# Global attention scores: three products of 64 rows, two key tiles at a time, in place of two products of 128 rows

## The chip, the cores and the metric

The kernel runs on one core of one Trainium2 chip. The metric is the device time of one execution in microseconds (us), and the time before is the median of three runs. PE is TensorE (PEld its weight loads), DVE is VectorE, ACT is ScalarE, POOL is GpSimd, SP is SyncE.

## The reference

One layer of a diffusion backbone over 1024 latent tokens and 256 context tokens, with 1024 channels. After a modulated projection there are two attention branches of 8 query heads and 2 key heads each (64 channels per head): branch A sees a window of 128 tokens to either side, branch B sees all 1024 latent keys, and both see the 256 context keys. A gated merge, a LayerNorm, a convolutional feed-forward block and a second LayerNorm follow. The part that the change touches is branch B:

```python
def _gqa_scores(q, k):
    return jnp.einsum("bqhgd,bkhd->bhgqk", q, k).astype(jnp.float32) * (HEAD_DIM ** -0.5)

def _global_attention(q, k_all, v_all):
    def one_block(i):
        q_blk = lax.dynamic_slice_in_dim(q, i * BLOCK, BLOCK, axis=1)
        p = jax.nn.softmax(_gqa_scores(q_blk, k_all), axis=-1)
        return _gqa_values(p, v_all)
```

Everything is float32.

## The kernel before

**Numbers in two parts.** Matrix products run on the type fp32r (`R32`), a float32 with a shortened mantissa. A float32 number is therefore split into a high part and a low part (`split`, L80): the high part is the rounded copy, and the low part is what is left. A product of two numbers then is high by high, high by low and low by high (`mm3`, L89: three matmuls), with low by low left out.

**Scores of the global branch.** A head has only 64 channels, so the high and the low part of a query fit one above the other on 128 rows. `qprep` (L479) makes two such tiles per unit: `q1` with the high part on rows 0 to 63 and the low part on rows 64 to 127, and `q2` with the two halves swapped. The keys lie the same way in `KL[h]` (128 rows, 1024 key columns; `KL[0]`, `KL[1]` for the windowed branch, `KL[2]`, `KL[3]` for the global one). `qk` (L494) then takes two matmuls of 128 rows, `q1` (L496) and `q2` (L497), and their sum holds all four products, low by low among them. One score tile `s` of a head has 1024 columns in two PSUM banks, so a head takes four matmuls of 512 columns (L520 and L521 call `qk` for each half).

**Units.** Attention is done in 32 units (`Unit`, L466): branch, block of 128 queries, group of four heads. Units 0 to 15 are windowed, 16 to 31 global. A global unit has `context` and `cxp` (scores against the context keys `KC`, tile `sx`, still with `qk`), four times `lat` (scores against the latent keys; then DVE scales them and takes the minimum, L545, and ACT takes the exponential, L547), and `value_steps`: transposes of the probabilities (L604, tile `ptr`), their split on ACT and DVE or POOL (L622, L623, L84, L87), and the products with the values (L634, L635, tile `av`). `self.kt` lists the key tiles in the order of the score columns, and `av_step` picks the value tile by it. Beside units 18 to 30 stand the matmuls of the first branch's output projection (tile `b`, L90 to L92). `s` has two buffers of two banks, `pt` (for `ptr`, `sx`, `b`) has three banks, `av` one.

**Keys.** `kv_post` (L423) prepares one tile of 128 tokens at a time: rotary embedding and norm, a split of all four key heads into `ks` on DVE (L450), four transposes on PE into `ktr` (L456), four copies into `KL` (L459, on ACT, for the last tile on DVE).

**A check inside the kernel.** In unit 3 of the windowed branch the kernel transposes one block of probabilities a second time as float32 (tile `both`, L609), copies it (L612), subtracts it from the first transpose (L613, tile `differ`) and adds the difference, times 1e30, to the unit's output (L655).

**What sets the order.** The projections up to the gates and the start of the merge are written in the order in which they run. From `loads.close()` (L832) on, keys and attention included, a scheduler decides the order of each engine's instructions from dependencies, priorities and its own costs; every engine then works through its list in that order. The stages behind attention come out in the same order before and after the change.

Of the kernel before, what the change touches and what calls it, by code (L numbers as in the profile page):

```python
# [7 lines left out]
F32 = mybir.dt.float32  # L8
R32 = mybir.dt.float32r
# [4 lines left out]
P = 128  # L14
# [55 lines left out]
def layer_kernel(  # L70
# [343 lines left out]
        q_evac(1, t, acc[t], bias_qb)  # L414

    KL, KC, VT = [], [], []

    def kv_alloc():
        KL.extend(ht(f"KL{h}", dt=R32) for h in range(4))
# [3 lines left out]
    def kv_post(t, kv):  # L423
        st = {}
        kb = kv[:, 128:256].rearrange("p (h d) -> p h d", d=HD)

        def s1():
            vt = VT[t // 2][:, t % 2]
            v3 = kv[:, 256:512].rearrange("p (h d) -> p h d", d=HD)
            nc.scalar.copy(vt[:, :, 0:HD], v3)  # L430
            tp = pw(f"ktp{t}")
            st["tp"] = tp = [tp[:, n * P:(n + 1) * P] for n in range(4)]
            st["ss"] = rms_scale(kb, 2, f"k{t}", tp[3])
            if t < NT:
                st["tb"] = ph1.tile([P, 2, HD], F32, tag="tb", name=f"tbk{t}", bufs=4)
                gfold(st["tb"], 1, t, nc.vector)
                rope(nc.vector, kv[:, 0:128], kv[:, 0:128], 2, ropec[:, t], ropes[:, t], f"ka{t}", tp[0], tp[1])
            nc.gpsimd.tensor_tensor(out=vt[:, :, HD:P], in0=v3, in1=vt[:, :, 0:HD].bitcast(F32), op=ALU.subtract)

        def s2():  # L440
            rms_apply(kb, 2, st["ss"])
            tp = st["tp"]
            if t < NT:
                tb = st["tb"]
                rope(nc.vector, kv[:, 128:256], kv[:, 128:256], 2, tb[:, 0], tb[:, 1], f"kb{t}", tp[2], tp[3])
            else:
                nc.gpsimd.tensor_tensor(out=kb, in0=kb, in1=bc(gcol[:, 1], 2), op=ALU.mult)
            st["ks"] = ks = pw(f"ks{t}", (P, 4, P), R32)
            k3 = kv[:, 0:256].rearrange("p (h d) -> p h d", d=HD)
            split(k3, ks[:, :, 0:HD], ks[:, :, HD:P], nc.vector, nc.vector)  # L450

        def s3():
            ks = st["ks"]
            tr = acc_tile(f"ktr{t}", R32).rearrange("p (h q) -> p h q", h=4)
            for h in range(4):
                nc.tensor.transpose(tr[:, h], ks[:, h], identr)  # L456
            if t < NT:
                for h in range(4):
                    (nc.vector.tensor_copy if t == NT - 1 else nc.scalar.copy)(KL[h][:, t * P:(t + 1) * P], tr[:, h])  # L459
            else:  # L460
                nc.scalar.copy(KC[0][:, :, (t - NT) * P:(t - NT + 1) * P], tr)
        return [s1] + [lambda: None] * GAP + [s2, s3]
# [3 lines left out]
    class Unit:  # L466
        def __init__(self, br, i, g):
            self.br, self.i, self.g = br, i, g
            self.id = f"{br}_{i}_{g}"
            if br == 1:  # L470
                self.k0, self.w, self.nc_ = 0, T, 2
                self.kt = list(range(10))
            else:
                w = [j for j in (i - 1, i, i + 1) if 0 <= j < NT]
                self.k0, self.w, self.nc_ = w[0] * P, len(w) * P, 1
                self.kt = w + [8, 9]
            self.n = br * 2 * NT + i * 2 + g
# [16 lines left out]
        def qk(self, o, h, ks, stop=True):  # L494
            hs = slice(h * P, (h + 1) * P)
            nc.tensor.matmul(o, self.q[0][:, hs], ks, start=True, stop=False)  # L496
            nc.tensor.matmul(o, self.q[1][:, hs], ks, start=False, stop=stop)  # L497

        def begin(self):
            self.nm = small(f"nm_{self.id}", (P, 4))  # L500
            self.sm = small(f"sm_{self.id}", (P, 4))
            self.other = negsink[:, self.g * 4:self.g * 4 + 4]
# [4 lines left out]
        def lat(self, h):  # L507
# [9 lines left out]
                self.qk(s[:, 256:512], h, KC[0][:, kh])  # L517
                o = s
            elif self.br == 1:
                for c in (0, 512):  # L520
                    self.qk(s[:, c:c + 512], h, KL[kh][:, c:c + 512])  # L521
                o = s
            else:
                w = self.w
# [70 lines left out]
        def value_steps(self):  # L595
# [5 lines left out]
            def tr_step(n):  # L601
# [2 lines left out]
                    i = nc.tensor.transpose(tr[:, h * P:(h + 1) * P], self.bits[:, h, n * P:(n + 1) * P], identr)  # L604
                    tc.add_manual_dep(i.ins, self.owner, data, reason="the row's words are read under another type")
                tr = tr.bitcast(F32)
                if nm == "0_3_0" and n == 0:
                    both = pt_tile("both")
                    i = nc.tensor.transpose(both[:, 0:P], self.bits[:, 0, 0:P].bitcast(F32), ident)  # L609
                    tc.add_manual_dep(i.ins, self.owner, data, reason="the row's words are read under another type")  # L610
                    self.differ = att.tile([P, P], F32, tag="rb", name="differ", bufs=2)
                    nc.vector.tensor_copy(self.differ, both[:, 0:P])  # L612
                    nc.vector.tensor_tensor(out=self.differ, in0=tr[:, 0:P], in1=self.differ, op=ALU.subtract)  # L613
                hi = att.tile([P, 512], R32, tag="pth", name=f"pth{nm}_{n}", bufs=4)
                lo = att.tile([P, 512], R32, tag="ptl", name=f"ptl{nm}_{n}", bufs=4)
                pooled = n in POOL_LO[self.br] and not last and (self.br or 2 <= 2 * self.i + self.g < 2 * NT - 3)
# [20 lines left out]
            def out_step():  # L637
# [13 lines left out]
                                     in0=low[0:HD].rearrange("p (a b q) -> p a b q", b=2, q=P)[:, :, h],  # L651
                                     in1=up.rearrange("p (a b q) -> p a b q", b=2, q=P)[:, :, h], op=ALU.add)
                (nc.vector if last else nc.gpsimd).tensor_tensor(out=ot, in0=ot, in1=self.rb, op=ALU.mult)
                if self.id == "0_3_0":
                    nc.vector.scalar_tensor_tensor(out=ot[:, 0], in0=self.differ, scalar=1e30, in1=ot[:, 0],  # L655
                                                   op0=ALU.mult, op1=ALU.add)
                hf = self.i // 4
                qs = slice((self.i % 4) * P, (self.i % 4 + 1) * P)
                split(ot, otile(self.br, hf, 0, self.g)[:, :, qs], otile(self.br, hf, 1, self.g)[:, :, qs],
# [1295 lines left out]
```

## Time and profile before

| | before |
|---|---|
| median of 3 runs (lowest to highest) | 1539.59 us (1539.46 to 1540.71) |
| profiled execution | 1539.04 us, of which the span of the trace is 1537.3 us |
| PE busy | 1510.2 us, 98% of the span |
| DVE, ACT, POOL busy | 77%, 51%, 49% of the span |
| global attention, units 16 to 31 | from 465 to 728 us of the span |

The profile is of one execution. Its page gives the busy time of each engine, the span in 40 slices, the chain of work that ended last, and the costliest groups of instructions; the trace behind it can be asked for single instructions, waits and windows of time. A matmul's duration in it includes its way through the array, so that neighbours overlap in time: what one matmul costs in a full stream is the distance from its start to the next one's start.

### The profile page before, as it was taken

To read this page: it belongs to the slowest core of one execution; us is meant where nothing else is said; L and a number is where in the kernel's file an instruction comes from. 1 tells how busy PE (TensorE), PEld (TensorE's weight loads), DVE (VectorE), ACT (ScalarE), POOL (GpSimd) and SP (SyncE) were. 2 spreads that over 40 slices of the span, in tenths; PEclk is the share of its full clock that TensorE was granted. 3 is DMA by queue.
4 is the path that set the end of the run, shared out by engine and by line. 5 is a ranking of instruction groups with operands and counts; after the bars stand their busy time and mean duration, and the time that the engine had idled before them with its cause. 6 is when DMAs were issued, how large, how long until landed. Compare 5 with 4: busy or idle time off the path is not lost.

```text
span 1537.3 us, 22216 instructions
## 1 busy us (share of the span) xinstructions
PE 1510.2 (98%) x7805; PEld 1265.8 (82%) x7805; DVE 1177.7 (77%) x1764; ACT 789.1 (51%) x1303; POOL 749.7 (49%) x727
## 2 busy tenths in 40 slices
PE   9999999999999999999999999999999999999997
PEld 7888888887787888887888998888888888888887
DVE  6677986538788788778865888888888888657884
ACT  5322222448888777677333554444444444435552
POOL 0356522415666777776223446666677774121121
PEclk9999999999999999999999999999999999999999
DMA  9777672322223677563550322333344447996721
GB/s 370 265 243 246 206 253 89 105 75 68 57 80 87 150 177 156 137 158 89 209 165 21 114 86 96 110 110 110 110 110 110 110 110 224 343 272 210 254 101 55
DMA packets 114399, 232.09 MB, mean 151 GB/s; under 512 B 13200, under 2 KB 28048, under 8 KB 114192
## 3 DMA queue, kind: packets, MB, share of 16 engines
q1 hardware_dynamic: 99056, 201.82, 39.3%
q0 software_dynamic: 10400, 20.19, 8.7%
q10 hardware_dynamic: 4832, 8.68, 1.5%
q8 instruction: 61, 1.00, 0.3%
q14 instruction: 50, 0.41, 0.1%
HBM read 179.45 MB, written 65.86 MB: 160 GB/s over the span
## 4 chain that ended last, share of the span: by engine, by line
PE 90%; POOL 3%; DVE 3%; ACT 2%; issue 2%; DMA 0%; SPq 0%; DVEq 0%; POOLq 0%; ACTq 0%
PE ptr L604 4%; PE p L90 4%; PE p L92 4%; PE p L91 4%; PE g L90 4%; PE g L92 4%; PE g L91 4%; PE av L634 3%; PE av L635 3%; PE b L90 3%; PE b L91 3%; PE b L92 3%; PE s L496 2%; PE s L497 2%; PE c L90 2%; PE c L91 2%
## 5 line engine op out<-in xcount | busy, mean ns | idle before, releaser
L623 DVE TENSOR_TENSOR ptl<-ptr,pth 128x512 fp32r<-128x512 f32 x195 | 128.8, 686 | 25.8 <-ACT pth L622 24.2
L547 ACT ACTIVATE p<-p,nm 128x1280 f32<-128x1280 f32 (+2 forms) x128 | 139.5, 1091 | 15.7 <-DVE p L545 14.6
L87 DVE TENSOR_TENSOR ld<-rd,hd 128x1024 fp32r<-128x1024 f32 x77 | 95.6, 1260 | 49.8 <-ACT hd L82 47.7
L622 ACT CAST pth<-ptr 128x512 fp32r<-128x512 f32 x195 | 110.9, 588 | 42.6 <-PE ptr L604 36.6
L82 ACT CAST hd<-rd 128x1024 fp32r<-128x1024 f32 x77 | 79.5, 1049 | 82.9 <-PE p L92 55.5
L604 PEld LDWEIGHTS ptr<-identr,pb 128*128 128x128 f32 x944 | 97.8, 141 | 22.6 <-ACT pb L550 3.1
L604 PE MATMUL ptr<-identr,pb 128*128 128x128 f32 x944 | 105.8, 243 | 2.3 <-ACT pb L550 1.3
L87 POOL TENSOR_TENSOR wlg<-wg,whg 128x512 fp32r<-128x512 f32 x32 | 46.8, 1471 | 123.6 <-ACT whg L82 84.8
L635 PE MATMUL av<-ptl,VT 128*128 128x512 f32 x236 | 98.3, 417 | 7.3 <-POOL ptl L87 7.1
L634 PE MATMUL av<-pth,VT 128*128 128x512 f32 x236 | 102.5, 434 | 2.7 <-ACT side L646 1.3
L90 PE MATMUL p<-hd 128*128 128x512 f32 x264 | 103.5, 392 | 0.0
L92 PE MATMUL p<-hd,ld 128*128 128x512 f32 x264 | 102.8, 389 | 0.0
L91 PE MATMUL p<-ld,hd 128*128 128x512 f32 x264 | 102.7, 389 | 0.0
L90 PE MATMUL g<-hh,whg 128*128 128x512 f32 x256 | 99.9, 390 | 0.0
L92 PE MATMUL g<-hh,wlg 128*128 128x512 f32 x256 | 99.6, 389 | 0.0
L91 PE MATMUL g<-hl,whg 128*128 128x512 f32 x256 | 99.6, 389 | 0.0
L545 DVE TENSOR_SCALAR_CACHE_REDUCE p<-s,cvt,nmc 128x1024 f32<-128x1024 f32 x64 | 84.1, 1317 | 8.2 <-PE s L497 8.1
L496 PE MATMUL s<-KL,q 128*128 128x512 f32 (+2 forms) x192 | 74.8, 389 | 1.2 <-DVE p L545 1.2
L497 PE MATMUL s<-KL,q 128*128 128x512 f32 (+2 forms) x192 | 72.5, 377 | 0.0
L793 ACT ACTIVATE sg<-g,bgc 128x512 f32<-128x512 f32 x32 | 22.0, 687 | 96.2 <-PE g L92 91.5
L82 ACT CAST wS<-s 128x512 fp32r<-128x512 f32 x76 | 45.3, 620 | 46.9 <-POOL s L1254 46.2
L82 ACT CAST wA<-ru 128x512 fp32r<-128x512 f32 x57 | 35.5, 623 | 63.6 <-PE d L92 34.8
(443 smaller groups left out, 4884.7 us busy)
## 6 DMA issues: line engine op xcount, KB each, us to landing
wml<-in_wmodT_dram SPq DMA_DIRECT2D x48, 512.0 KB
ru<-in_w_up_dram SPq DMA_DIRECT2D x38, 512.0 KB
rd<-td SPq DMA_DIRECT2D x55, 256.0 KB
rd<-sd SPq DMA_DIRECT2D x44, 256.0 KB
rd<-in_w_dn_dram SPq DMA_DIRECT2D x33, 256.0 KB
wm<-in_wmodT_dram SPq DMA_DIRECT2D x16, 512.0 KB
wg<-in_w_g_dram SPq DMA_DIRECT2D x32, 256.0 KB
sgd<-sg ACTq DMA_DIRECT2D x32, 256.0 KB
```

The lines of the kernel that those rows point to most:

```text
L82: nc.scalar.copy(hi, src)
L87: lo_eng.tensor_tensor(out=lo, in0=src, in1=hi.bitcast(F32), op=ALU.subtract)
L90: nc.tensor.matmul(ps, a[0], b[0], start=start, stop=False, skip_group_check=resumed)
L91: nc.tensor.matmul(ps, a[0], b[1], start=False, stop=False, skip_group_check=resumed)
L92: nc.tensor.matmul(ps, a[1], b[0], start=False, stop=stop, skip_group_check=resumed)
L496: nc.tensor.matmul(o, self.q[0][:, hs], ks, start=True, stop=False)
L547: nc.scalar.activation(row, row, AF.Exp, bias=self.nm[:, hs], scale=-1.0, accum_out=self.sm[:, hs])
L604: i = nc.tensor.transpose(tr[:, h * P:(h + 1) * P], self.bits[:, h, n * P:(n + 1) * P], identr)
L622: nc.scalar.copy(hi, tr)
L623: nc.vector.tensor_tensor(out=lo, in0=tr, in1=hi.bitcast(F32), op=ALU.subtract)
L634: nc.tensor.matmul(self.av, v, hi, start=first, stop=False)
L635: nc.tensor.matmul(self.av, v, lo, start=False, stop=self.left == 0)
```

## The change

The latent scores of the global branch are formed from 64 rows at a time. `KL[2]` and `KL[3]` get another layout: rows 0 to 63 hold the even key tiles (0, 2, 4, 6), rows 64 to 127 the odd ones, columns 0 to 511 their high parts, columns 512 to 1023 their low parts. `qk_rows` issues six matmuls of 64 rows by 512 columns for one head. They go by turns: one on the upper rows (into the first bank of `s`), one on the lower rows (into the second bank), three times over: high query by high key, low query by high key, high query by low key. Low by low is left out. `q1` and `q2` stay as they are, since each has a high part on one half and a low part on the other. `self.kt` follows the new order of score columns. Context scores and the windowed branch keep `qk`.

For the new layout, the split of a latent key tile becomes two (two heads into `ks`, two into a new tile `kp` that holds two neighbouring key tiles), the four transposes become two per tile and four more after every odd tile (tile `ktp`), and the copies change from four of 128 columns per tile to two per tile and two of 256 columns per pair. The memory that the framework sets aside for descriptors of DMAs, until now left at its default, is set to 8192 bytes per partition (`dynamic_dma_scratch_size`). The check inside the kernel (`both`, `differ`) is taken out.

```diff
+    kp = [None]
...
             k3 = kv[:, 0:256].rearrange("p (h d) -> p h d", d=HD)
+            if t < NT:
+                if t % 2 == 0:
+                    kp[0] = ph1.tile([P, 2, 2, 2, HD], R32, tag="kp", name=f"kp{t}", bufs=2)
+                st["kp"] = kp[0]
+                split(k3[:, 2:4], kp[0][:, :, 0, t % 2], kp[0][:, :, 1, t % 2], nc.vector, nc.vector)
+                k3, ks = k3[:, 0:2], ks[:, 0:2]
             split(k3, ks[:, :, 0:HD], ks[:, :, HD:P], nc.vector, nc.vector)
...
-            for h in range(4):
+            for h in range(2 if t < NT else 4):
                 nc.tensor.transpose(tr[:, h], ks[:, h], identr)
             if t < NT:
-                for h in range(4):
-                    (nc.vector.tensor_copy if t == NT - 1 else nc.scalar.copy)(KL[h][:, t * P:(t + 1) * P], tr[:, h])
+                cp = nc.vector.tensor_copy if t == NT - 1 else nc.scalar.copy
+                for h in range(2):
+                    cp(KL[h][:, t * P:(t + 1) * P], tr[:, h])
+                if t % 2:
+                    m = slice(t // 2 * P, (t // 2 + 1) * P)
+                    tr = acc_tile(f"ktp{t}", R32).rearrange("p (h a q) -> p h a q", h=2, a=2)
+                    for h in range(2):
+                        for a in range(2):
+                            nc.tensor.transpose(tr[:, h, a], st["kp"][:, h, a].rearrange("p a d -> p (a d)"), identr)
+                    for h in range(2):
+                        cp(KL[2 + h].rearrange("p (a k) -> p a k", a=2)[:, :, m], tr[:, h])
...
-                self.kt = list(range(10))
+                self.kt = [0, 2, 4, 6, 1, 3, 5, 7, 8, 9]
...
+        def qk_rows(self, s, h, k):
+            q1, q2 = (t[:, h * P:(h + 1) * P] for t in self.q)
+            for n, (hi, c) in enumerate(((1, 0), (0, 0), (1, HALF))):
+                for a in range(2):
+                    r = slice(a * HD, (a + 1) * HD)
+                    nc.tensor.matmul(s[:, a * HALF:(a + 1) * HALF], (q1 if a != hi else q2)[r], k[r, c:c + HALF],
+                                     start=n == 0, stop=n == 2)
...
-                for c in (0, 512):
-                    self.qk(s[:, c:c + 512], h, KL[kh][:, c:c + 512])
+                self.qk_rows(s, h, KL[kh])
...
-                if nm == "0_3_0" and n == 0:
-                    both = pt_tile("both")
...
-                if self.id == "0_3_0":
-                    nc.vector.scalar_tensor_tensor(out=ot[:, 0], in0=self.differ, scalar=1e30, in1=ot[:, 0],
-                                                   op0=ALU.mult, op1=ALU.add)
...
-    nc = _bacc.Bacc("TRN2", target_bir_lowering=False, num_devices=1)
+    nc = _bacc.Bacc("TRN2", target_bir_lowering=False, num_devices=1, dynamic_dma_scratch_size=8192)
```

In the program this looks as follows. The first place is PE at the first head of global unit 3_0 (`s1_3_0_0` is that head's score tile, `q11` and `q21` its two query tiles, `ptr` and `av` belong to the values of the unit before). Before:

```order
L635 MATMUL av1_2_0_6010<-ptl1_2_0_8_6137,VT4_2139 128x512
L496 MATMUL s1_3_0_0_6187<-KL2_2132,q11_3_0_5895 128x512
L497 MATMUL s1_3_0_0_6187<-KL2_2132,q21_3_0_5896 128x512
L496 MATMUL s1_3_0_0_6187<-KL2_2132,q11_3_0_5895 128x512
L497 MATMUL s1_3_0_0_6187<-KL2_2132,q21_3_0_5896 128x512
L604 MATMUL ptr1_2_1_2_6194<-identr_59,pb1_2_1_6075 128x128 x4
```

And after; a row with x2 stands for two matmuls in a row, the first on one half of the rows, the second on the other:

```order
L520 MATMUL s1_3_0_0_6245<-KL2_2132,q11_3_0_5945 128x512
L520 MATMUL s1_3_0_0_6245<-KL2_2132,q21_3_0_5946 128x512 x2
L520 MATMUL s1_3_0_0_6245<-KL2_2132,q11_3_0_5945 128x512 x2
L520 MATMUL s1_3_0_0_6245<-KL2_2132,q21_3_0_5946 128x512
L627 MATMUL ptr1_2_1_2_6254<-identr_59,pb1_2_1_6133 128x128 x4
```

Four matmuls became six, and the six stand together between the same neighbours. So it is for 43 of the 64 heads. At the other 21 the scheduler puts matmuls of 128 rows between the six; the second place is PE at the first head of unit 2_1, where `b` is the output projection of the other branch. Before:

```order
L634 MATMUL av1_1_1_5779<-pth1_1_1_7_5871,VT3_2138 128x512
L496 MATMUL s1_2_1_0_5973<-KL3_2133,q11_2_1_5680 128x512
L497 MATMUL s1_2_1_0_5973<-KL3_2133,q21_2_1_5681 128x512
L604 MATMUL ptr1_1_1_9_5909<-identr_59,pb1_1_1_5639 128x128 x4
L496 MATMUL s1_2_1_0_5973<-KL3_2133,q11_2_1_5680 128x512
```

After:

```order
L520 MATMUL s1_2_1_0_6023<-KL3_2133,q11_2_1_5722 128x512
L650 MATMUL av1_1_1_5823<-pth1_1_1_8_5955,VT4_2139 128x512
L627 MATMUL ptr1_2_0_0_5983<-identr_59,pb1_2_0_5904 128x128 x4
L520 MATMUL s1_2_1_0_6023<-KL3_2133,q21_2_1_5723 128x512 x2
L627 MATMUL ptr1_2_0_1_5992<-identr_59,pb1_2_0_5904 128x128 x4
L651 MATMUL av1_1_1_5823<-ptl1_1_1_8_5956,VT4_2139 128x512
L90 MATMUL b0_3_0_6009<-O0000_3284,hwb0_3_0_5933 128x512
```

Here the six are broken into groups of one, two and three (the three follow behind the twelve matmuls of `b`). Over the program the 384 matmuls of 64 rows stand in 89 unbroken groups: 41 of six, one of twelve, eight of five, four of four, thirteen of three, nine of two and thirteen single ones.

The third place is DVE in the windowed branch, where the check was. Before, between the minima of unit 3_1 (`p0_3_1`) and the low parts of unit 3_0 (`ptl0_3_0`):

```order
L545 TENSOR_SCALAR p0_3_1_3824,nm_0_3_1_3822<-s0_3_1_1_3859,negsink_63 128x640
L612 COPY differ_3832<-both_3830 128x128
L545 TENSOR_SCALAR p0_3_1_3824,nm_0_3_1_3822<-s0_3_1_2_3867,negsink_63 128x640
L613 TENSOR_TENSOR differ_3832<-ptr0_3_0_0_3825,differ_3832 128x128
L545 TENSOR_SCALAR p0_3_1_3824,nm_0_3_1_3822<-s0_3_1_3_3883,negsink_63 128x640
```

After:

```order
L568 TENSOR_SCALAR p0_3_1_3840,nm_0_3_1_3838<-s0_3_1_1_3870,negsink_63 128x640
L639 TENSOR_TENSOR ptl0_3_0_0_3847<-ptr0_3_0_0_3841,pth0_3_0_0_3846 128x512
L639 TENSOR_TENSOR ptl0_3_0_1_3867<-ptr0_3_0_1_3861,pth0_3_0_1_3866 128x512
L568 TENSOR_SCALAR p0_3_1_3840,nm_0_3_1_3838<-s0_3_1_2_3878,negsink_63 128x640
L568 TENSOR_SCALAR p0_3_1_3840,nm_0_3_1_3838<-s0_3_1_3_3894,negsink_63 128x640
```

The copy and the subtraction are gone, two low parts stand earlier, and the scheduler orders units 3_0 to 4_0 anew on every engine.

More of the change, by code (lines that the diff above doesn't have):

```diff
@@ L606, in tr_step @@
                 tr = tr.bitcast(F32)
-                if nm == "0_3_0" and n == 0:
-                    both = pt_tile("both")
[L609 to L613, printed above, removed]
                 hi = att.tile([P, 512], R32, tag="pth", name=f"pth{nm}_{n}", bufs=4)
```

## The prediction, made before the changed kernel ran

> **What bounds the kernel now.** I read the page first. In the slices a digit is the busy share in tenths, and PEclk is the clock granted to PE.
>
> ```profile
> span 1537.3 us, 22216 instructions
> PE   9999999999999999999999999999999999999997
> DVE  6677986538788788778865888888888888657884
> PEclk9999999999999999999999999999999999999999
> ```
>
> PE is busy at full clock everywhere. "Busy" alone doesn't bound a stage, so next come the busy times in two windows (PE, PEld, DVE, ACT, POOL): a plain stream of matmuls, and the global attention.
>
> ```profile
> 100.00:200.00 100.00, 100.00 (x443) 82.81 (x442) 81.11 (x126) 25.35 (x41) 60.04 (x51) 1.00 0.70 235
> 466.00:720.00 254.00, 252.66 (x1550) 207.58 (x1548) 206.94 (x407) 185.94 (x322) 182.90 (x233) 1.00 0.59 139
> ```
>
> In the 254 us of global attention PE stands idle for 1.34 us. DVE works 207 of 254 (81%), ACT 73%, POOL 72%. Then the waits in that stage: who waited for whom, us in total, times, longest.
>
> ```profile
> ACT side L619 <- PE ptr L604: 26.7, 24, 3.7
> ACT pth L622 <- PE ptr L604: 25.7, 34, 2.0
> PEld av L634 <- ACT side L646: 3.7, 13, 1.0
> PE ptr L604 <- ACT pb L550: 0.7, 2, 0.4
> ```
>
> The others wait for PE, and PE for nobody to speak of. Whatever PE is spared here shortens the span until another engine is late.
>
> **The scores now.** The groups of the latent scores, and one head from the timeline (start, duration):
>
> ```profile
> L496 PE MATMUL s<-KL,q 128*128 128x512 f32 x128 | 51.6, 403 | 0.0
> L497 PE MATMUL s<-KL,q 128*128 128x512 f32 x128 | 51.2, 400 | 0.0
> 592.53 0.39 PE L496 MATMUL s<-KL,q 128*128 128x512 f32 x1
> 592.76 0.39 PE L497 MATMUL s<-KL,q 128*128 128x512 f32 x1
> 592.99 0.39 PE L496 MATMUL s<-KL,q 128*128 128x512 f32 x1
> 593.22 0.39 PE L497 MATMUL s<-KL,q 128*128 128x512 f32 x1
> 593.44 0.43 PE L634 MATMUL av<-pth,VT 128*128 128x512 f32 x1
> ```
>
> A matmul lasts 0.39 us, but the next starts 0.23 us later: 0.23 us is its price in a stream. The 256 matmuls cost 256 x 0.23 = 58.9 us of PE.
>
> **The scores after.** There are 384 matmuls of 64 rows. All have 512 columns, so each still streams as long; the change pays only if one on the upper and one on the lower rows run at the same time. No matmul of 64 rows stands in this trace, so I bound this from both sides.
>
> - Upper end: they run one after the other, as all matmuls in the rows above do. 384 x 0.23 = 88.3 us, +29.4 us.
> - Lower end: both halves of a pair start together. A group broken by 128-row work takes half its matmuls, rounded up. The 89 groups of the order make 41 x 3 (sixes) + 6 (the twelve) + 8 x 3 (fives) + 4 x 2 (fours) + 13 x 2 (threes) + 9 (twos) + 13 (singles) = 209 turns. 209 x 0.23 = 48.1 us, -10.8 us. (Unbroken, 192 turns would give -14.7 us.)
> - Between: weights must be loaded for each of the six. Their pace shows where matmuls are short, at the context scores (PEld rows):
>
> ```profile
> 563.50 0.19 PEld L497 LDWEIGHTS sx<-KC,q 128*128 128x128 f32 x1
> 563.62 0.19 PEld L496 LDWEIGHTS sx<-KC,q 128*128 128x128 f32 x1
> 563.74 0.19 PEld L497 LDWEIGHTS sx<-KC,q 128*128 128x128 f32 x1
> 563.85 0.19 PEld L496 LDWEIGHTS s<-KL,q 128*128 128x128 f32 x1
> ```
>
> One starts each 0.117 us, two take 0.23 us: just the time of a pair. The loads keep up, but the second half of a pair can start up to half a turn late. Then every group has half a turn more than its length, (384 + 89) / 2 = 236.5 turns, 54.4 us, -4.5 us.
>
> I take -8 us, a little nearer to the lower end than the middle (-7.7), since loads run ahead of the matmul they serve and both halves of a group's first pair can be loaded in time.
>
> **The edges.** Each of the 89 groups is entered from 128-row work and left to it: 178 changes of shape that were not there. The nearest row is `str`, a weight tile of 4 columns amid full ones:
>
> ```profile
> 596.57 0.39 PE L496 MATMUL s<-KL,q 128*128 128x512 f32 x1
> 596.80 0.27 PE L567 MATMUL str<-ident,sm 128*4 128x128 f32 x1
> 596.83 0.48 PE L497 MATMUL s<-KL,q 128*128 128x512 f32 x1
> 597.14 0.40 PE L496 MATMUL s<-KL,q 128*128 128x512 f32 x1
> 333.06 0.22 PE L514 MATMUL s<-maskr,identr 128*128 128x128 f32 x1
> 333.12 0.34 PE L496 MATMUL s<-KC,q 128*128 128x256 f32 x1
> 333.29 0.28 PE L497 MATMUL s<-KC,q 128*128 128x256 f32 x1
> ```
>
> From 596.57 to 597.14 are 0.57 us, less two matmuls of 0.23: `str` costs 0.11 us. An ordinary 128-column matmul, the mask (333.06 to 333.29, less 0.117 for the 256 columns behind it), costs 0.11 too. So a narrower weight tile costs nothing at its two edges. The other end: the array must be empty at an edge, and the tail of a matmul, 0.39 - 0.23 = 0.16 us, is paid each time: 178 x 0.16 = 28.5 us. I take 0, the nearest row, and keep 28.5 as the first rival. The Trainium skill, TensorEngine Tiling (Array Packing), section Tiling Modes, Key Properties, says that changing the tiling mode drains TensorE; by that rule the edges cost and the sum would be the first rival's. The `str` rows show no such drain, but whether 4 columns count as another mode no row tells.
>
> **The rest.** The check on DVE in the windowed branch:
>
> ```profile
> 390.57 0.29 DVE L612 COPY differ<-both 128x128 f32<-128x128 f32 x1 [0.87 <-POOL O L84]
> 392.40 0.28 DVE L613 TENSOR_TENSOR differ<-ptr,differ 128x128 f32<-128x128 f32 x1
> 407.68 0.69 DVE L655 SCALAR_TENSOR_TENSOR ot<-differ,ot 128x128 f32<-128x128 f32 x1 [0.72 <-POOL ot L653]
> ```
>
> Its work and the waits ahead of it come to 0.87 + 0.29 + 0.28 + 0.72 + 0.69 = 2.85 us of DVE, in a stage in which PE does wait:
>
> ```profile
> 380.00:400.00 20.00, 16.32 (x108) 13.60 (x108) 15.03 (x34) 14.31 (x34) 11.44 (x19) 1.00 0.17 37
> 400.00:420.00 20.00, 19.26 (x137) 17.03 (x137) 16.69 (x36) 17.09 (x42) 13.55 (x21) 1.00 0.26 73
> ```
>
> PE is idle for 4.4 of these 40 us. I take -1 us out of 0 to -2.85; the new order of units 3_0 to 4_0 may add or take 1.5 us.
>
> The keys, prepared beside a full PE:
>
> ```profile
> 250.00:332.00 82.00, 82.00 (x388) 67.91 (x387) 41.63 (x138) 27.40 (x75) 26.33 (x31) 1.00 0.27 87
> L86 DVE CAST ks<-kv 128x256 fp32r<-128x256 f32 x10 | 2.9, 289 | 0.6 <-POOL kv L447 0.5
> L459 DVE CAST KL<-ktr 128x128 fp32r<-128x128 f32 x4 | 0.9, 283 | 22.7 <-PE ktr L456 22.7
> ```
>
> DVE gets 16 more instructions of about 0.28 us, 4.5 us, in 82 us in which it works 42 and PE is covered by the gates' matmuls: nothing. Transposes stay 40. The last tile's four copies (0.88 us, ahead of the first minimum) become two and two wider ones; without cover at most +0.3 us.
>
> Smaller descriptor memory can only matter where POOL issues DMAs:
>
> ```profile
> L1014 POOL DMA_DIRECT2D sd<-in_w_dn_dram x12 | 14.2, 1186 | 18.9 <-DMA sd<-sd 12.2 <-DMA sd<-in_w_dn_dram 5.4 <-DVE p L559 1.1
> ```
>
> An issue takes 1.2 us and PE did not wait for POOL in the list of waits above; were each of the 12 to take twice as long, 14 us of POOL fit into its 71 idle us. Nothing, at most +1 us.
>
> With 8 us less of PE, DVE's 207 us stand in 246 (84%): still behind PE, though some waits will be longer, +0.5 us. What is late next is DVE's minimum, with two score tiles in turn.
>
> **Sum.** -8 - 1 + 0.5 = -8.5 us, from the profiled 1539.04 us (span 1537.3 and 1.74 around it) to 1530.5. The median of 1539.59 lies 0.55 above the profiled time, so the forecast is 1531.0. Its own range: -10.8 - 2.85 - 1.5 gives 1524.4, and -4.5 + 1.5 + 1 + 0.3 gives 1537.9.
>
> **Rivals.**
>
> 1. *The edges cost: slower.* Place: the 178 changes between 64-row and 128-row matmuls. From 8.5 / 178 = 0.048 us per edge the gain is gone. At half the tail, 0.08 us, +14.2 - 8.5 = +5.7, 1545.3; at the whole tail, +28.5 - 8.5, 1559.6. For: the scheduler breaks 21 heads into pieces, and the loads at an edge may not run ahead. Against: the `str` rows. Chance 0.16.
> 2. *The halves don't overlap*, the change doing what it says but not what could pay: +29.4 - 0.5 = +28.9, 1568.5. For: no two matmuls of this trace run together at full length. Against: the two products of a pair share neither rows nor a PSUM bank. Chance 0.10.
> 3. *A pair is slower than one matmul: no difference.* At 58.9 / 209 = 0.28 us per pair instead of 0.23, or with half of it lost to DVE's waits besides, PE gains nothing and about 1539 remains; up to 0.27 us per pair it is 1537. For: two loads fill a turn to the last nanosecond (0.234 of 0.23 us). Chance 0.10. The Trainium skill, TensorE: Matmul & The Clock Gate, section Measured speedup vs the span model, gives 3.07 times for four matmuls of 32 rows; as an estimate of mine, the same loss on two halves is a factor of 1.53 (2 x 3.07 / 4), 384 x 0.23 / 1.53 = 57.7 us, a gain of 1.2 us. No run here shows it yet.
>
> **How the numbers follow.** The forecast has 0.64, the rivals 0.16, 0.10 and 0.10. Faster by over 0.2% (3.1 us, about what a measurement of this kernel can tell from no change) is the forecast, 0.64; within 0.2% is rival 3, 0.10; slower are rivals 1 and 2, 0.26. The range runs from 1524 over the forecast and rival 3 to the lower half of rival 1, 1546; left out are rival 2 and rival 1's upper half, 0.18.
>
> **What would show it.** Right: the two L520 matmuls of a pair start within some hundredths of a us of each other and the next pair 0.23 us later; the matmul behind a head starts as after any other; the global attention is about 8 us shorter with PE still idle for under 4 us. Rival 1: inside a group 0.23 us per pair, but a gap ahead of and behind it. Rival 2: starts 0.23 us apart, one by one. Rival 3: pairs more than 0.25 us apart. Wrong altogether if the time moves elsewhere: in the windowed stage by more than 3 us, or behind attention, where the order is as before.

## The result: 1560.2 us, slower by 1.35%

The changed kernel took 1560.2 us (median of 4 runs, 1560.05 to 1560.57), beside 1539.55 us for the kernel before on the same chip. The ratio is 1.0135, 95% interval 1.0123 to 1.0147: 20.65 us slower where I had forecast 8.6 us faster. The time is that of rival 1, the edges, at its full price (1559.6). The times below are medians of executions in the fast state; one execution far off, 6119.69 us of the kernel with a short matmul of 128 rows, is left out (its median is 1551.32 without it and 1551.71 with it).

First the page of the changed kernel. Its columns are those of the rows quoted in the prediction.

```profile
span 1558.5 us, 22489 instructions
PE   9999999998999999999999999999999999999997
PEclk9999999999999999999999999999999999999999
L520 PE MATMUL s<-KL,q 64*128 64x512 f32 x384 | 72.2, 436 | 0.0
```

By these digits the granted clock and PE's busy share are as before. The one group of 384 matmuls has 72.2 us of busy time, less than the 51.6 + 51.2 of the two groups that it replaces, so by this list the change worked. The list misleads: a matmul in it has a modelled end, and an empty array ahead of a matmul is no busy time of any group. What a matmul costs is the time from its start to the next start, and that has to be read from the timeline.

So next the ends of the global attention: the first context score and the last value product on PE, of before and then of after.

```profile
464.91 0.28 PE L496 MATMUL sx<-KC,q 128*128 128x256 f32 x1
...
733.35 0.39 PE L635 MATMUL av<-ptl,VT 128*128 128x512 f32 x1
```

```profile
462.99 0.28 PE L512 MATMUL sx<-KC,q 128*128 128x256 f32 x1
...
754.63 0.39 PE L651 MATMUL av<-ptl,VT 128*128 128x512 f32 x1
```

The stage lasted 268.4 us and lasts 291.6: 23.2 us more. (The table of before let it end at 728 us; its last value product starts at 733.35.) It starts 1.9 us earlier. 23.2 - 1.9 = 21.3, and the span grew by 21.2 (1537.3 to 1558.5). The whole loss lies in this stage, and nothing behind it changed.

Most of the earlier start is no effect of the change. The column behind POOL's busy time is the granted clock; the first row is of before, the second of after:

```profile
338.00:344.00 6.00, 5.24 (x29) 4.58 (x29) 3.00 (x9) 4.05 (x12) 0.94 (x1) 0.72 0.57 174
338.00:344.00 6.00, 5.32 (x40) 4.50 (x40) 3.87 (x12) 5.13 (x15) 2.15 (x4) 1.00 0.56 177
```

In the profiled execution of before PE ran for 3.4 us at half the clock, from 340.06 us on. Beside the kernel without the check, whose matmuls start at the same times up to there, it is 1.23 us late at 344 us. The slices of a page are too coarse to show this.

The busy times in the same window as in the prediction (PE, PEld, DVE, ACT, POOL):

```profile
466.00:720.00 254.00, 249.86 (x1533) 178.97 (x1531) 189.84 (x368) 171.64 (x297) 167.26 (x212) 1.00 0.55 129
```

DVE, ACT and POOL each do about 8% less in these 254 us (DVE 206.94 before, 189.84 now), because they are fed more slowly. PE is not short of work: it stands idle for 4.1 us. PE became slower at its own work.

Where, the timeline of PE shows (start, duration; x6 is an unbroken group of six matmuls), with the weight loads (PEld) of the same stretch below:

```profile
601.33 0.46 PE L650 MATMUL av<-pth,VT 128*128 128x512 f32 x1
601.64 0.40 PE L651 MATMUL av<-ptl,VT 128*128 128x512 f32 x1
601.96 0.96 PE L520 MATMUL s<-KL,q 64*128 64x512 f32 x6
602.86 0.88 PE L627 MATMUL ptr<-identr,pb 128*128 128x128 f32 x8
603.58 0.35 PE L512 MATMUL sx<-KC,q 128*128 128x256 f32 x1
```

```profile
601.40 0.19 PEld L651 LDWEIGHTS av<-ptl,VT 128*128 128x128 f32 x1
601.96 0.53 PEld L520 LDWEIGHTS s<-KL,q 64*128 64x128 f32 x6 [0.37 <-issue]
602.86 0.74 PEld L627 LDWEIGHTS ptr<-identr,pb 128*128 128x128 f32 x8 [0.37 <-issue]
```

Three things stand here. From the `av` at 601.64 to the scores are 0.32 us instead of the 0.23 of a stream. The six take 0.90 us to the next start where three turns are 0.70. And PEld, which otherwise runs ahead of the matmul it serves, stands idle for 0.37 us at both edges and starts only with the matmuls themselves: weights of the other height are not loaded beside running matmuls. At all 174 recorded edges of this kernel the first load and its matmul start within 0.004 us of each other. The list of waits has this for the whole stage (us, times, longest), with "issue" for a wait whose cause the profile does not see:

```profile
PEld s L520 <- issue: 16.7, 49, 0.4
PEld ptr L627 <- issue: 11.6, 36, 0.4
```

Before, the loads of scores and transposes waited in this way for 0.2 us in all. By the length of the group, the time from its first start to what follows it is, as the median over the stage: single matmuls 0.42 us, two 0.43, three 0.66, six 0.89, the twelve 1.60. That is 0.19 + 0.235 us for each pair, rounded up. So the halves do run beside each other, completely: the two matmuls of a group's first pair start 0.003 us apart. The single starts, which the rows above merge, show where a group pays: 0.09 us ahead of it, whatever stands there; 0.10 between its first pair and its second (0.336 us instead of 0.235); 0.09 behind its last pair; and then 0.03 more in the first matmul behind it if that is a transpose, 0.10 if it has 512 columns. Together that is 0.31 to 0.38 us a group.

### The profile page after: what moved, and what is told of

The parts are those of the page before. It is cut to its first block, busy times and chain, and to the rows that moved or that the text cites. A ratio compares the mean times of both kernels' runs of the same rounds, so it can differ in the third digit from the quotient of the medians.

```text
span 1558.5 us, 22489 instructions
## 1 busy us (share of the span) xinstructions
PE 1528.2 (98%) x7932; PEld 1251.6 (80%) x7932; DVE 1176.2 (75%) x1777; ACT 788.3 (51%) x1295; POOL 747.1 (48%) x727
## 4 chain that ended last, share of the span: by engine, by line
PE 87%; POOL 4%; DVE 3%; ACT 3%; issue 2%; DMA 0%; SPq 0%; DVEq 0%; POOLq 0%; ACTq 0%
PE ptr L627 4%; PE p L90 4%; PE p L92 4%; PE p L91 4%; PE g L90 4%; PE g L91 4%; PE g L92 4%; PE av L650 3%; PE b L90 3%; PE s L520 3%; PE b L91 3%; PE b L92 3%; PE av L651 3%; PE c L90 2%; PE c L91 2%; PE d L91 2%
## 5 line engine op out<-in xcount | busy, mean ns | idle before, releaser
L87 DVE TENSOR_TENSOR ld<-rd,hd 128x1024 fp32r<-128x1024 f32 x77 | 94.8, 1249 | 51.2 <-ACT hd L82 49.0
L627 PEld LDWEIGHTS ptr<-identr,pb 128*128 128x128 f32 x944 | 93.8, 140 | 33.3 <-issue 11.6
L627 PE MATMUL ptr<-identr,pb 128*128 128x128 f32 x944 | 109.2, 248 | 2.2 <-DVE ptl L639 1.4
L92 PE MATMUL p<-hd,ld 128*128 128x512 f32 x264 | 102.8, 389 | 0.0
L91 PE MATMUL p<-ld,hd 128*128 128x512 f32 x264 | 102.8, 389 | 0.0
L520 PE MATMUL s<-KL,q 64*128 64x512 f32 x384 | 72.2, 436 | 0.0
L568 DVE TENSOR_SCALAR_CACHE_REDUCE p<-s,negsink 128x640 f32<-128x640 f32 (+1 forms) x64 | 53.2, 845 | 12.5 <-PE s L513 11.9
```

Source lines behind the costliest of these rows:

```text
L87: lo_eng.tensor_tensor(out=lo, in0=src, in1=hi.bitcast(F32), op=ALU.subtract)
L91: nc.tensor.matmul(ps, a[0], b[1], start=False, stop=False, skip_group_check=resumed)
L92: nc.tensor.matmul(ps, a[1], b[0], start=False, stop=stop, skip_group_check=resumed)
L520: nc.tensor.matmul(s[:, a * HALF:(a + 1) * HALF], (q1 if a != hi else q2)[r], k[r, c:c + HALF], start=n == 0, stop=n == 2)
L568: nc.vector.tensor_scalar(out=out, in0=o, scalar1=self.qscale(nqs)[:, hs] if self.br else -1.0, scalar2=self.other[:, hs], op0=ALU.mult, o ...
```

## The experiments

All are compared with the kernel before on the same chip. Sums by kind of matmul are mine: for each row of PE's timeline from the first context score to the last value product, the time from its start to the next row's start.

**One matmul more, of 128 rows and of 64.** Both are the kernel before, without its check, with a short matmul ahead of each of the 64 heads of global attention; the second differs in the one slice.

```diff
                for c in (0, 512):
-                    self.qk(s[:, c:c + 512], h, KL[kh][:, c:c + 512])
+                hs = slice(h * P, (h + 1) * P)
+                i = nc.tensor.matmul(s[:, 0:P], self.q[1][0:P, hs], KL[kh][0:P, 0:P], start=True, stop=True)
+                with tc.issue_after(i.ins):
+                    for c in (0, 512):
+                        self.qk(s[:, c:c + 512], h, KL[kh][:, c:c + 512])
```

The second has `0:HD` for both `0:P`.

> The kernel before, with one more matmul of 128 rows and 128 columns ahead of the scores of each of the 64 global heads (its result is overwritten). Edge theory (each change between 64-row and 128-row matmuls costs PE time, 0.29 us per group and up to 0.38 us with what follows it): no change of shape here, so only the matmul itself, 64 x 0.11 = 7 us, 1546 to 1548. Order theory (the loss comes from the new order and from late engines): the order hardly differs from before, the same 7 us.

> The same program and the same order on every engine as the one with the 128-row matmul, only that the added matmul takes 64 rows. Edge theory: 64 groups of one, 64 x 0.29 to 0.38 us = 18.6 to 24.3 us more than with 128 rows, 1565 to 1572. Order theory: within 1 us of the 128-row version.

Measured: 1551.32 with 128 rows (ratio 1.0076, 1.0061 to 1.0092) and 1567.02 with 64 (1.0176, 1.0162 to 1.0190). The added matmul of 128 rows cost 12.0 us where I had expected 7. Making it of 64 rows, with nothing else changed and PE's rows in the stage in the same order, cost another 15.7 us, 0.25 us for each of the 64 groups; I had expected 18.6 to 24.3. One head of each, first with 128 rows, then with 64:

```profile
559.84 0.39 PE L631 MATMUL av<-ptl,VT 128*128 128x512 f32 x1
560.07 0.22 PE L521 MATMUL s<-KL,q 128*128 128x128 f32 x1
560.13 0.45 PE L496 MATMUL s<-KL,q 128*128 128x512 f32 x1
560.42 0.40 PE L497 MATMUL s<-KL,q 128*128 128x512 f32 x1
```

```profile
565.41 0.40 PE L631 MATMUL av<-ptl,VT 128*128 128x512 f32 x1
565.74 0.32 PE L521 MATMUL s<-KL,q 64*128 64x128 f32 x1
565.99 0.50 PE L496 MATMUL s<-KL,q 128*128 128x512 f32 x1
566.33 0.39 PE L497 MATMUL s<-KL,q 128*128 128x512 f32 x1
```

Start to start: 0.23, 0.06 and 0.29 us in the first, 0.33, 0.25 and 0.34 in the second. The edges cost 0.10 ahead of the short matmul, 0.19 behind it and 0.05 once more, 0.34 us in all at this head. This kernel has no halves and no pairs, so the price is that of the change of height alone. Over the 62 recorded heads the row ahead of the short matmul, the short one and the row behind it take 19.7 us more with 64 rows than with 128, 0.32 us a head. All the other rows of the stage together take 6 us less, which is why the net price is lower; why they do stays open.

**The same matmul with fewer columns.** My prediction had taken its price for an edge from a tile of 4 columns. So the added matmul, in the same kernel without its check, got a weight tile of all 128 rows and 64 columns.

```diff
-                i = nc.tensor.matmul(s[:, 0:P], self.q[1][0:P, hs], KL[kh][0:P, 0:P], start=True, stop=True)
+                i = nc.tensor.matmul(s[0:HD, 0:P], self.q[1][:, h * P:h * P + HD], KL[kh][:, 0:P], start=True, stop=True)
```

> The kernel before with the added matmul ahead of each of 64 heads as before, but its weight tile is of all 128 rows and 64 columns (the added one of 128 x 128 gave 1551.7, the one of 64 rows and 128 columns 1567.0; order and length of the moving side are the same in all three). If fewer columns also change the shape and drain the array: about 1567, within 2. If only fewer rows do (the transposes with a tile of 128 rows and 4 columns, which showed no price, are of this kind): 1551 to 1553, the time with 128 x 128.

Measured: 1552.29 (ratio 1.0090, 1.0073 to 1.0106), the time with 128 x 128. The rows at a head:

```profile
558.64 0.40 PE L631 MATMUL av<-ptl,VT 128*128 128x512 f32 x1
558.88 0.22 PE L521 MATMUL s<-KL,q 128*64 128x128 f32 x1
558.94 0.45 PE L496 MATMUL s<-KL,q 128*128 128x512 f32 x1
559.23 0.40 PE L497 MATMUL s<-KL,q 128*128 128x512 f32 x1
```

0.24, 0.06 and 0.29 us, no edge. Fewer columns cost nothing that shows; fewer rows do. The `str` rows were the wrong neighbour.

**The check left out.** The kernel before without the lines of the check in the windowed branch, which the change removes too.

```diff
-                if nm == "0_3_0" and n == 0:
-                    both = pt_tile("both")
...
-                if self.id == "0_3_0":
-                    nc.vector.scalar_tensor_tensor(out=ot[:, 0], in0=self.differ, scalar=1e30, in1=ot[:, 0],
-                                                   op0=ALU.mult, op1=ALU.add)
```

> The kernel before without the check in unit 3 of the windowed branch. Edge theory says nothing of it; the milestones of the two traces put the windowed stage 1.9 us shorter after the change, so -1.9 us, 1537.7. Order theory, by which the windowed stage gained through the other edits: no change, 1539.6.

Measured: 1538.79 (ratio 0.9996, 0.9988 to 1.0005), not to be told from no change; the 1.9 us that I had put on it are not there.

**Not by turns.** The changed kernel with the three matmuls of the upper rows first and then the three of the lower.

```diff
-            for n, (hi, c) in enumerate(((1, 0), (0, 0), (1, HALF))):
-                for a in range(2):
+            for a in range(2):
+                for n, (hi, c) in enumerate(((1, 0), (0, 0), (1, HALF))):
```

> The changed kernel with the three upper matmuls of a head first and then the three lower ones. If only neighbours in the queue overlap, a head has five turns instead of three (the third upper one still meets the first lower one): 64 x 2 x 0.235 = 30 us more, 1585 to 1595. If halves overlap wherever they stand, or if they don't overlap at all, no change, 1560.

Measured: 1565.65 (ratio 1.0168, 1.0153 to 1.0184), only 5.5 us over the changed kernel. My expectation of some 30 us was wrong. A group of two and a group of six of this kernel, each with what follows, and then a group of two of the changed kernel:

```profile
475.20 0.73 PE L520 MATMUL s<-KL,q 64*128 64x512 f32 x2
475.86 1.22 PE L627 MATMUL ptr<-identr,pb 128*128 128x128 f32 x12
...
482.76 0.97 PE L520 MATMUL s<-KL,q 64*128 64x512 f32 x6
483.66 0.88 PE L627 MATMUL ptr<-identr,pb 128*128 128x128 f32 x8
```

```profile
475.03 0.50 PE L520 MATMUL s<-KL,q 64*128 64x512 f32 x2
475.47 1.21 PE L627 MATMUL ptr<-identr,pb 128*128 128x128 f32 x12
```

Six in the order upper, upper, upper, lower, lower, lower take the same 0.90 us, and start two by two, the two of a pair 0.01 us apart. The lower ones must have started while upper ones issued earlier were still waiting: strictly in the order of issue the first lower one could start only with the third upper one, five turns in all, and with 0.19 for the group the six would have taken 5 x 0.235 + 0.19 = 1.37 us. The rest of PE's order is that of the changed kernel, row by row. Only where a group is broken into pieces of one height does the order count: two of the same half take 0.66 us, one of each 0.44.

**Fewer edges: six or twelve kept together.** The changed kernel with the six matmuls of a head issued one right behind the other (56 groups instead of 89), and with those of two heads together (32 groups).

```diff
-                    nc.tensor.matmul(s[:, a * HALF:(a + 1) * HALF], (q1 if a != hi else q2)[r], k[r, c:c + HALF],
-                                     start=n == 0, stop=n == 2)
...
+            with tc.high_priority():
+                last = one(*todo[0])
+                for t in todo[1:]:
+                    with tc.issue_after(last):
+                        last = one(*t)
```

Within a head both kernels take low query by high key first. The kernel with twelve takes the score tile of the next head ahead of time (`self.pair`), puts both heads' matmuls in `todo`, and waits for both tiles at the first.

> The changed kernel with the six matmuls of a head kept together: 56 groups instead of 89, 192 turns instead of 209. Edge theory, at 0.36 us per group: 33 x 0.36 + 17 x 0.235 = 16 us less than the changed kernel, about 1544. Order theory (late engines, not edges, make the loss): some other order of the same work, 1556 to 1564.

> The changed kernel with the matmuls of two heads kept together: 32 groups of twelve. Edge theory: 57 x 0.36 + 17 x 0.235 = 24.5 us less than the changed kernel, 1535.7, and up to 1541 if waiting for both score tiles at once costs. Order theory: worse than with groups of six, since a group waits for two score tiles, over 1556.

Measured: 1552.64 (ratio 1.0084, 1.0070 to 1.0098) and 1550.66 (1.0066, 1.0053 to 1.0080). Fewer edges are faster than 1560.2, but by 7.6 and 9.5 us, about half of what I had expected or less. Either an edge costs less than I thought, or keeping matmuls together has a price of its own.

**No edge, and six kept together.** Issued in the same way as with six, but each matmul of 128 rows and 256 columns: six of these stream as long as three pairs. The scores are then one product over part of the keys.

```diff
-                        todo.append((s[:, a * HALF:(a + 1) * HALF], (q1 if a != hi else q2)[r], k[r, c:c + HALF], n))
+                        m = a * HALF + n % 2 * 256
+                        todo.append((s[:, m:m + 256], q1 if a != hi else q2, k[:, m:m + 256], n))
```

> The kernel with groups of six, but each of the six takes 128 rows and 256 columns, so that it streams as long per head as three perfect pairs (6 x 0.117 us) without any change of shape; the scores are one product only and so not the reference's. Edge theory: 64 x (0.93 - 0.70) = 15 us less than before and 1.9 us of the windowed stage, 1523 to 1529. Order theory: no better than with groups of six in 64 rows.

Measured: 1537.33 (ratio 0.9986, 0.9977 to 0.9996). Against the kernel with six of 64 rows that is -15.3 us for 56 groups, 0.27 us each, though the scheduler's order on PE differs between the two. But against the kernel before it is only 2 us, far from the 1523 to 1529 expected, though the scores on PE fell from 60.1 to 45.5 us by my sums; the stage stayed at 268.4. The window, and the waits of PE and PEld in the stage:

```profile
466.00:720.00 254.00, 246.39 (x1668) 208.31 (x1666) 204.69 (x403) 187.34 (x323) 182.56 (x231) 1.00 0.59 138
```

```profile
PE av L662 <- POOL ptl L87: 3.4, 4, 1.4
...
PEld av L662 <- POOL ptl L87: 4.8, 4, 1.7
```

PE is idle for 7.6 of 254 us, and its longest wait is for POOL's low parts. So either the other engines eat whatever PE is spared, and my forecast was wrong in a second step, or the forced order makes them late. The last three kernels were made for this.

**Keeping together alone.** The kernel before, with its own four matmuls of a head kept together by the same means.

```diff
-                for c in (0, 512):
-                    self.qk(s[:, c:c + 512], h, KL[kh][:, c:c + 512])
+                last = None
+                with tc.high_priority():
+                    for c in (0, 512):
+                        for n in range(2):
+                            with tc.issue_after(last) if last is not None else _nullcontext():
+                                last = nc.tensor.matmul(s[:, c:c + 512], self.q[n][:, hs], KL[kh][:, c:c + 512],
+                                                        start=n == 0, stop=n == 1).ins
```

> The kernel before, with the four score matmuls (128 rows, 512 columns) of each global head issued one right behind the other instead of spread over the scheduler's order; nothing else is changed and no work is added or left out. It asks what keeping a head's score matmuls together costs by itself, since the kernels with six or twelve kept together came out at 1552.6 and 1550.7 and the one with six short matmuls at 1537.3. If only the changes of weight shape cost (theory of the edges): 1539.6 within 2. If keeping them together makes the other engines late (rival: the order): 1544 to 1552, with TensorE waiting for the exponents' splits and for its transposes' inputs as in the kernel with twelve.

Measured: 1544.33 (ratio 1.0031, 1.0019 to 1.0042), 4.9 us slower with the same matmuls. In the window PE is now idle for 3.0 us; the rows below it, from the timeline, are the first context score and the last value product of the stage:

```profile
466.00:720.00 254.00, 251.01 (x1521) 206.49 (x1521) 201.07 (x395) 185.11 (x318) 178.95 (x227) 1.00 0.60 139
```

```profile
462.92 0.35 PE L496 MATMUL sx<-KC,q 128*128 128x256 f32 x1
...
735.90 0.39 PE L641 MATMUL av<-ptl,VT 128*128 128x512 f32 x1
```

The stage lasts 272.98 us, 4.5 more than the 268.44 before; what this execution gains ahead of it (2.0) it loses behind it (2.4). The forced order has a price of its own. It is probably part of what the kernels with six and twelve lost, and of the 12.0 us of the added short matmul: its own 62 recorded matmuls come to 5.0 us by my sums and the scores behind them take 2.7 more, 7.7 in all, near the 7 expected.

**No edge, loose order.** The changed kernel in its own order, each of its six matmuls made one of 128 rows and 256 columns.

```diff
             for n, (hi, c) in enumerate(((1, 0), (0, 0), (1, HALF))):
                 for a in range(2):
-                    r = slice(a * HD, (a + 1) * HD)
-                    nc.tensor.matmul(s[:, a * HALF:(a + 1) * HALF], (q1 if a != hi else q2)[r], k[r, c:c + HALF],
-                                     start=n == 0, stop=n == 2)
+                    m = a * HALF + n % 2 * 256
+                    nc.tensor.matmul(s[:, m:m + 256], q1 if a != hi else q2, k[:, m:m + 256],
+                                     start=True, stop=True)
```

> The changed kernel in its own loose order, with each of its six score matmuls made one of 128 rows and 256 columns: the time of the scores on TensorE is about that of three ideal pairs (6 x 0.117 = 0.70 us a head, 3 x 0.235) and the weight shape never changes. The scores are then one product only over part of the keys, so the output isn't the reference's; nothing else is left out. Theory (the edges were the loss, and TensorE's freed time is the span's): 1539.6 - 13 = 1526 to 1530. Rival (TensorE's freed time is taken by waits for other engines, as in the kernel with six short ones kept together): 1536 to 1540. Should it be near 1528 while the one kept together was 1537.3, keeping together cost 9.

Measured: 1530.84 (ratio 0.9947, 0.9933 to 0.9960), 8.5 us faster than before, a little over the 1526 to 1530 of the theory, and 29.4 us faster than the changed kernel. The page's span, the window, the ends of the stage, and the longest waits of PE in it:

```profile
span 1530.4 us, 22434 instructions
```

```profile
466.00:720.00 254.00, 247.95 (x1702) 213.15 (x1701) 209.17 (x411) 191.49 (x334) 185.38 (x235) 1.00 0.59 139
```

```profile
462.90 0.28 PE L512 MATMUL sx<-KC,q 128*128 128x256 f32 x1
...
725.20 0.39 PE L651 MATMUL av<-ptl,VT 128*128 128x512 f32 x1
```

```profile
PE av L651 <- POOL ptl L87: 1.5, 2, 0.9
PE ptr L627 <- ACT pb L573: 1.4, 3, 0.6
```

The stage lasts 262.3 us, 6.1 less than before and 29.3 less than in the changed kernel, and begins 2.0 earlier than before, of which some 1.2 are the stretch of lower clock. PE is idle for 6.1 of 254 us instead of 1.3: of the scores' gain about half is lost, most of it to later inputs. This is the changed kernel without its edges, and it takes the time that I had forecast for it. But the scheduler gave its stage another order on PE, so the 29.4 us hold that order too; only the two kernels with one short matmul, of 128 x 128 and of 64 rows, differ in the edges alone. Behind the stage this execution loses 1.3 us again, at places that the change does not touch; why stays open.

**One step less on POOL.** The last kernel with `POOL_LO = (3,), (2,)` instead of `(3,), (2, 6)`.

> The same kernel with one of the two key steps per unit of the global attention whose split of the weights goes by way of GpSimd given to ScalarE and VectorE like the rest. If GpSimd's queue (behind its accumulating transfers) is what took the freed time of TensorE: 3 to 8 us faster than the kernel with the same matmuls and both steps on GpSimd. If VectorE or ScalarE is the next bound: 2 to 6 us slower than that, since each of 16 steps adds 0.6 us or more to VectorE.

Measured: 1540.86 (ratio 1.0008, 1.0000 to 1.0017), 10 us slower than with both steps on POOL. Taking this work off POOL doesn't help, so its share of the split on POOL is not what holds the span; the direction is that of the rival, the size more than the 2 to 6 us that I gave it. In the window PE is idle for 11.6 us while POOL works 32 us less and DVE 3 us more:

```profile
466.00:720.00 254.00, 242.45 (x1663) 208.46 (x1661) 211.89 (x417) 185.11 (x321) 153.78 (x201) 1.00 0.59 138
```

Whether DVE alone makes the 10 us, or the scheduler's new order with it, these runs don't tell.

## Why the prediction was wrong, step by step

**The edges: the step that failed.** "I take 0, the nearest row." The nearest row was one of fewer columns; the change has fewer rows. With one short matmul the two were told apart: 64 columns cost nothing against 128 x 128 (1552.29 and 1551.32), 64 rows cost 14.7 to 15.7 us. In the changed kernel the price is 1560.2 - 1530.84 = 29.4 us (28.9 by the ratios, (1.0135 - 0.9947) x 1539.5) for 178 changes, 0.165 us each. The trace of the changed kernel alone gives nearly the same: the rows just ahead of its groups take 8.6 us more than their usual step, the scores 16.3 more than the 48.6 of the kernel without edges, the rows just behind 3.4 more, 28.3 us for 87 recorded groups. Rival 1 had put it at 0.16 us an edge, the tail of a matmul that must have left the array, 28.5 us in all. That its number is met so well is partly luck: of its 0.16 us the trace shows 0.09 ahead of the first matmul behind an edge, and the rest (0.10, or 0.03 at a transpose) between that matmul, whose load was not done ahead, and the next. In the kernels with one group a head the net price is 0.23 to 0.27 us a group instead of 0.33. In the one of 64 rows the rows at the heads do pay 0.32 us; the difference is what the rest of the stage got back.

The Trainium skill, TensorEngine Tiling (Array Packing), section Tiling Modes, Key Properties, says that a change of the tiling mode drains TensorE. The traces agree for rows as far as they show it, with 0.09 us ahead of each edge and 0.33 us a group in all, and I had weighed that rule lightly against a row that did not bear on it. The 64-column tile paid nothing; whether the array changed its mode for it no run shows.

**The scores.** "209 turns x 0.23 us ... -10.8 us" was right as the lower end: 0.235 us a pair, and the kernel without edges, whose matmuls stream for about as long, has 48.6 us of scores. The half turn by which a second half might start late (-4.5) doesn't exist; I took -8 out of caution. The rivals "no overlap" and "a pair slower than one matmul" fall: in groups of six the two halves run beside each other all the time. The fear that two loads just fill a turn was a wrong reading too: the two loads of a pair start 0.004 us apart, one for each half, and the next two 0.11 us later. My estimate from the Trainium skill, TensorE: Matmul & The Clock Gate, section Measured speedup vs the span model (a gain of 1.2 us) was too low for such a stream: two halves together are twice as fast as one after the other inside a group.

**PE bounds the stage, the others are behind it.** Right, as far as it went: without edges the span follows PE for about half of what PE is spared. The term was too small. I took +0.5 us for longer waits; in the kernel without edges the scores fell by 11.5 us and the stage by 6.1, so 5.4 were lost. That -8 - 1 + 0.5 met the time of that kernel to 0.2 us is then partly luck: -11.5 + 5.4 - 2.0 is the sum that was measured to the end of the stage, and some 1.2 of the 2.0 are the stretch of lower clock in the trace of before.

**The check, the keys, the descriptor memory.** Small, as taken. The check alone moved the kernel by -0.5 us of which nothing is certain, where I had taken -1. The changed kernel starts the stage 1.9 us earlier, but the kernel that only keeps four matmuls together, check and all, starts it 2.0 earlier too (462.92), and two kernels without the check, those with a short matmul of 128 x 128 and of 64 rows, whose traces have the same stretch of lower clock (0.72 from 338 to 344 us), start it at 464.58 and 464.76. So most of the earlier start follows the clock and not the check; my reading of the digits, "at full clock everywhere", missed that stretch. Behind the stage nothing moved: its end is 21.3 us later, the span 21.2 longer.

**The likely mechanism of the edge.** PEld's idle 0.37 us ahead of the loads of the other height shows that weights of 64 rows are not loaded while matmuls of 128 rows run, nor the other way round. So the load and the wait ahead of it stand open on PE each time. That the 0.09 us ahead are the array running empty and the 0.10 behind the load is likely by their places, but no run separates them.

## What to carry to other kernels

By these prices matmuls of 64 rows on two halves can pay only in long groups: here a head's group of six saves one turn of 0.23 us and pays 0.33 us for being entered and left. Groups of twelve, which save two turns, were slower than before all the same (1550.66); an order that keeps a head's matmuls together cost about 5 us by itself. No kernel of this study with all its attention work done is faster than the one before by more than the noise. When a cost has no row, ask whether the nearest row differs in the same dimension (rows against columns), and try that first: one short matmul ahead of each head would have decided this case.

## What the hardware showed that I had not expected

- A matmul of 64 rows amid ones of 128 costs 0.10 us ahead of it and 0.24 behind it at the head shown; one of 64 columns amid 128 costs nothing that shows.
- The halves of the array go through their own matmuls independently: six take 0.90 us whether they are issued by turns or three and three. In the unbroken twelve the two starts of a pair drift from 0.003 us apart to 0.047.
- Weights for the two halves load side by side: the two loads of a pair start 0.004 us apart and the first two pairs 0.11 us apart, where loads of 128 rows start 0.117 us apart one by one. A load itself is no shorter (0.18 us, and 0.19 with 128 rows).
- Busy time by group can fall (102.8 to 72.2 us) while the stage gets longer by 23.2 us.
- A few us at half clock, hidden in the slices of a page, moved a milestone of one profiled execution by over 1 us.
